# Modulation rows on another queue and in other places, and several orders of issue, in a two-layer trunk

## The chip, the cores and the metric

The kernel runs on one core of a Trainium2 chip. The metric is the device time of one execution in microseconds: three timed runs of the kernel before gave 3098.6, 3098.68 and 3101.12, median 3098.68. One more execution was taken with the profiler on. A core has a matmul engine (TensorE, PE in the profile; its weight loads are PEld), VectorE (DVE), ScalarE (ACT), GpSimd (POOL) and a queue engine (SyncE, SP) that here only starts transfers. Each engine runs its own instructions in the order written for it; transfers started by SP, ScalarE and GpSimd stand in one queue for each of them.

## The reference, cut to what matters

512 tokens of width 1024 pass a recurrent layer and an attention layer, each followed by a layer of small experts. Six vectors of 1024 for each of the two layers, and two for the shared keys and values, come from a condition vector and modulate the norms and the residuals:

```python
mod = (silu(c) @ ada_w[l] + ada_b[l])          # sh1, sc1, g1, sh2, sc2, g2
h = rmsnorm(x, norm_mix_g[l]) * (1.0 + sc1) + sh1
# l = 0: rglru_block: gate, rec = split(h @ w_in); xc = conv(rec)
#   r, i = sigmoid(xc @ wa + ba), sigmoid(xc @ wx + bx)
#   a = exp(-8 * r * softplus(-lam)); b = sqrt(1 - a**2) * i * xc
#   y = (gelu(gate) * scan(a, b)) @ w_out
# l = 1: mla_block, with keys and values from the same x and their own shift and scale
x = x + g1 * y
h = rmsnorm(x, norm_ffn_g[l]) * (1.0 + sc2) + sh2
x = x + g2 * peer(h)     # 8 heads: scores, top 16 of 128 x 128 experts, gelu(h.u), sum of v
```

## The kernel before, in words

Everything is kept transposed: 8 chunks of 128 features by 512 tokens. Matmuls work in three passes on a high and a low half of each operand. A weight tile is loaded by SP into a buffer `raw` (4 of them, L171 to L175), copied by ScalarE to its high half `whi` (3 buffers, L162), and what is left is subtracted to the low half `wlo` (3 buffers, L163), on VectorE or GpSimd.

The 14 vectors are 112 modulation rows of 128 x 1024 weights (0.5 MB each). `ada` (L143 to L152) loads a row on SP's queue and multiplies it with the condition on VectorE, which sums it to one column of `mod`. `adas(n)` takes the next n rows of the list `todo`. Rows 0 to 23 are done in the first products of the recurrent layer.

The order of the instructions on each engine is found by a planner that issues what is ready in its own timing, earlier program lines first. `issue_after(i)` puts what is traced under it, on the engine of `i`, behind `i`; `high_priority` puts it ahead of all else that is ready.

*Recurrent layer (`rglru`).* The record product (w_rec, 8 steps of 24 matmuls) runs while rows and norms are made; then gate products (w_in, L393 to L396), the convolution on VectorE (L384 to L389), gates and decays (L398 to L421). After two heads, the four roots are taken on ScalarE (L440), and products, scans and gates follow on VectorE (L442 to L449). 6 rows are put behind the convolution, 10 behind the last split. The output product (w_out, L454 to L463) ends with 8 residuals, squares and sums of squares; the sums (`nacc`, L226) are all on VectorE, and TensorE then adds them over the features (L232).

*Expert layer (`peer`).* Four score groups (pq) with top-16 searches on VectorE; 5 rows behind each in layer 0, 2 in layer 1, and expert products u (24 matmuls each) in between. Then 24 gate groups, 8 for each of three token blocks: one-hot matrices on VectorE and their matmuls (wps, L856). The gate tiles of the next block come from `decode` in 7 steps, the last of which ends in `gate_prep`. The fourth token block is done by gathers (L1146) on GpSimd's queue and VectorE, spread over all that follows. The value stage takes 128 steps: gate products on VectorE (L1020), splits of activations and of a value tile, 18 matmuls into six accumulators (`acc`); from step 84 on an expert product runs beside each step. In layer 0, rows are taken at every third step from step 2 on, up to row 67 (24 rows), and the rotary angles are computed at step 2 in the gathers' buffers. The last three steps are held back: first half, then second half in two parts with residuals between (`finish`).

*Attention (`mla`).* 16 heads; two rows after each head from the fourth on, up to row 87 (20 rows). The output product of each four heads adds a residual with rows 64 to 71. Layer 1's score groups take the last 8 rows.

## Time and profile before

| | us |
|---|---|
| median of three timed runs | 3098.68 |
| profiled execution, its own time | 3100.75 |
| its span, first to last instruction | 3098.8 |
| PE busy | 2980.4 (96%) |
| DVE busy | 2557.2 (83%) |
| ACT busy | 1381.6 (45%) |
| POOL busy | 860.2 (28%) |

The times in a profile are microseconds from the start of the span. A view by stretches gives, for each, its length, the busy time of each engine with its count of instructions, the granted clock of TensorE (1.00 is full) and what the transfers did. A view in order of time gives start, duration, engine, line, operation, output and inputs; in square brackets stands how long the engine had been idle before and what ended it. A view of waits gives the engine and line that waited, for whom, the sum, how often and the longest. The stages lie at: recurrent layer 0 to 212, score groups to 480, gate groups to about 790, value stage to 1500, attention to 1800, then the same expert stages to 3085.

### The profile page before, as it was taken

How to read it: one execution, taken by the hardware profiler on the slowest of the kernel's cores; microseconds unless marked ns; L12 is line 12 of the kernel's file. 1: busy time of each engine (PE TensorE's matmuls, PEld its weight loads, DVE VectorE, ACT ScalarE, POOL GpSimd, SP SyncE). 2: the span in 40 equal slices, each digit the busy share in tenths (PEclk: the TensorE clock that was granted, in tenths of full speed). 3: DMA queues.
4: the chain of work that ended last, by engine and by line, in shares of the span. 5: the costliest groups of instructions: out<-in, count | busy, mean ns of one | idle time of the engine just before them, and what ended most of it. 6: DMA issues, size and time to landing. Idle time of an engine off the chain costs nothing.

```text
span 3098.8 us, 43500 instructions
## 1 busy us (share of the span) xinstructions
PE 2980.4 (96%) x15516; PEld 2642.5 (85%) x15516; DVE 2557.2 (83%) x4841; ACT 1381.6 (45%) x1974; POOL 860.2 (28%) x667
## 2 busy tenths in 40 slices
PE   7889999999999999999899989999999999999998
PEld 5569999999877889998677779999999788889997
DVE  8789999898787878888767778999886787778886
ACT  5543255655333333333566642455554333333333
POOL 4000003343212215544333300014432221134441
PEclk9999999999999999999999999999999999999999
DMA  8344568999999999999313244469998999999994
GB/s 307 125 160 150 170 201 309 313 344 325 360 309 360 347 329 343 344 338 340 102 48 114 81 150 138 133 228 332 314 337 310 365 353 313 323 317 343 335 334 154
DMA packets 345047, 821.01 MB, mean 265 GB/s; under 512 B 33600, under 2 KB 179136, under 8 KB 338432
## 3 DMA queue, kind: packets, MB, share of 16 engines
q1 hardware_dynamic: 239632, 460.91, 44.2%
q0 software_dynamic: 73728, 268.47, 24.5%
q10 hardware_dynamic: 31472, 88.87, 7.4%
q8 instruction: 122, 2.00, 0.3%
q14 instruction: 93, 0.76, 0.1%
HBM read 730.85 MB, written 87.29 MB: 264 GB/s over the span
## 4 chain that ended last, share of the span: by engine, by line
PE 82%; DVE 7%; DMA 6%; issue 3%; ACT 2%; POOL 1%; DVEq 0%; ACTq 0%; SPq 0%; POOLq 0%
PE u L187 11%; PE u L188 11%; PE u L189 11%; PE acc L188 10%; PE acc L187 10%; PE acc L189 10%; PE wps L856 6%; PE pq L187 2%; PE pq L188 2%; PE pq L189 2%; DMA vraw<-in_v_dram 2%; DMA ada_raw<-in_adaw_dram 2%; DVE ada_junk L151 1%; PE sc L963 1%; DVE wlo L163 1%
## 5 line engine op out<-in xcount | busy, mean ns | idle before, releaser
L1146 POOL DMA_INDIRECT grow<-in_u_dram,idx x256 | 348.7, 1362 | 1280.0 <-DVE gdot L1150 441.0
L187 PE MATMUL u<-hh,wlo 128*128 128x384 f32 x2048 | 691.8, 338 | 1.5 <-ACT gsp L917 1.5
L189 PE MATMUL u<-hh,whi 128*128 128x384 f32 x2048 | 688.1, 336 | 0.0
L188 PE MATMUL u<-hl,whi 128*128 128x384 f32 x2048 | 686.6, 335 | 0.0
L188 PE MATMUL acc<-vl,ah 128*128 128x512 f32 x1536 | 598.6, 390 | 1.4 <-DVE vl L163 1.4
L189 PE MATMUL acc<-vh,ah 128*128 128x512 f32 x1536 | 598.4, 390 | 0.0
L187 PE MATMUL acc<-vh,al 128*128 128x512 f32 x1536 | 539.2, 390 | 17.7 <-ACT vh L162 9.1
L1146 POOL DMA_INDIRECT grow<-in_v_dram,idx x256 | 365.4, 1427 | 685.7 <-DVE gacc L1155 405.9
L163 DVE TENSOR_TENSOR wlo<-raw,whi 128x1024 fp32r<-128x1024 f32 x315 | 383.4, 1219 | 115.7 <-ACT whi L162 114.0
L163 DVE TENSOR_TENSOR vl<-vraw,vh 128x1024 fp32r<-128x1024 f32 x256 | 313.2, 1224 | 150.6 <-ACT vh L162 139.6
L162 ACT ACTIVATE whi<-raw 128x1024 fp32r<-128x1024 f32 (+2 forms) x372 | 358.6, 965 | 146.8 <-PE wo L189 27.7
L187 PEld LDWEIGHTS u<-hh,wlo 128*128 128x128 f32 x2048 | 386.5, 189 | 4.7 <-ACT gsp L917 1.8
L188 PEld LDWEIGHTS u<-hl,whi 128*128 128x128 f32 x2048 | 385.9, 188 | 2.7
L189 PEld LDWEIGHTS u<-hh,whi 128*128 128x128 f32 x2048 | 385.3, 188 | 0.0
L187 PEld LDWEIGHTS acc<-vh,al 128*128 128x128 f32 x1536 | 289.0, 189 | 80.8 <-ACT vh L162 11.3
L188 PEld LDWEIGHTS acc<-vl,ah 128*128 128x128 f32 x1536 | 289.4, 188 | 60.9 <-DVE vl L163 2.0
L189 PEld LDWEIGHTS acc<-vh,ah 128*128 128x128 f32 x1536 | 289.2, 188 | 59.7
L1155 DVE SCALAR_TENSOR_TENSOR gacc<-grow,gdot,gacc 128x1024 f32<-128x1024 f32 x254 | 324.8, 1279 | 12.2 <-DMA grow<-in_v_dram,idx 10.0
L162 ACT ACTIVATE vh<-vraw 128x1024 fp32r<-128x1024 f32 x256 | 268.9, 1051 | 141.1 <-DMA vraw<-in_v_dram 55.2
L1150 DVE CUSTOM_DVE_ANT_0 grow<-grow,hn 128x1024 f32<-128x1024 f32 x256 | 308.9, 1219 | 15.5 <-DMA grow<-in_u_dram,idx 15.4
L162 ACT ACTIVATE ah<-gact 128x384 fp32r<-128x384 f32 x180 | 94.1, 523 | 331.2 <-PE acc L189 168.8
L859 ACT ACTIVATE stg<-wps 128x512 f32<-128x512 f32 x192 | 187.7, 1110 | 49.2 <-PE wps L856 44.8
(352 smaller groups left out, 4203.5 us busy)
## 6 DMA issues: line engine op xcount, KB each, us to landing
raw<-in_uT_dram SPq DMA_DIRECT2D x256, 512.0 KB
vraw<-in_v_dram SPq DMA_DIRECT2D x256, 512.0 KB
ada_raw<-in_adaw_dram SPq DMA_DIRECT2D x112, 512.0 KB
wscr<-stg ACTq DMA_DIRECT2D x48, 1024.0 KB
wt<-wscr SPq DMA_DIRECT2D x32, 1536.0 KB
gscr<-gsp ACTq DMA_DIRECT2D x152, 192.0 KB
gact<-gscr SPq DMA_DIRECT2D x110, 192.0 KB
raw<-in_w_pq_dram SPq DMA_DIRECT2D x32, 512.0 KB
```

Source lines behind the costliest of these rows:

```text
L151: nc.vector.tensor_tensor_reduce(junk, raw, self.csil, op0=OP.mult, op1=OP.add, scale=1.0, scalar=b, accum_out=col)
L162: nc.scalar.activation(hi, src, AF.Copy)
L163: return (eng or nc.vector).tensor_tensor(lo, src, hi.bitcast(F32), op=OP.subtract)
L187: nc.tensor.matmul(out, al, bh, start=first, stop=False)
L188: nc.tensor.matmul(out, ah, bl, start=False, stop=False)
L189: return nc.tensor.matmul(out, ah, bh, start=False, stop=last)
L856: last = nc.tensor.matmul(wps[:, t * P:t * P + P], oo[:, n4 + a, :, t], pr[:, q * n4 + a, :, t], start=q == 0, stop=q == 1)
L859: nc.scalar.activation(stg[:, :, c:c + 4].rearrange("p e t -> p t e"), wps.rearrange("p (t e) -> p t e", t=4), AF.Copy, scale=1.0 / GSCALE)
L963: nc.tensor.matmul(sc[:, m * P:m * P + P], qs[m][:, b * P:b * P + P], keys[:, m, :], start=True, stop=True)
L1146: nc.gpsimd.indirect_dma_start(out=row, out_offset=None, in_=tabs[s], in_offset=bass.IndirectOffsetOnAxis(ap=idx[:, k:k + 1], axis=0))
L1150: nc.vector.tensor_tensor_reduce(row, row, hn, op0=OP.mult, op1=OP.add, scale=1.0, scalar=0.0, accum_out=col)
L1155: nc.vector.scalar_tensor_tensor(acc, row, col, acc, op0=OP.mult, op1=OP.add)
```

## The change

Rows: `ada` and `adas` get a queue; the 16 rows of the recurrent layer after the first 24 are loaded on GpSimd's queue, 8 behind the convolution and 8 behind the last split (before: 6 and 10 on SP's). Score groups of layer 0 take 6 rows instead of 5. In the value stage of layer 0 none is taken before step 64, then one every third step up to row 63 (16 rows, steps 66 to 111). So attention takes rows 64 to 87. The first two w_in tiles are loaded and split at high priority. The product after each root stands behind the last `a` of the decays. Four sums of squares of the recurrent layer go to GpSimd. The decode steps run one gate group ahead. The splits of value tiles 1 and 2 stand behind their step's gate product. The last three value steps of the second half are put so that five of the eight residuals stand between them (before: four).

```diff
-    def ada(self, n, pool=None, bufs=2):
+    def ada(self, n, pool=None, bufs=2, queue=None):
...
-        nc.sync.dma_start(raw, self.io["adaw"][n])
+        (queue or nc.sync).dma_start(raw, self.io["adaw"][n])
...
-            win = [self.wtile(io["w_in"][m], KC, eng=nc.vector) for m in range(2)]
+            with tc.high_priority():
+                win = [self.wtile(io["w_in"][m], KC, eng=nc.vector) for m in range(2)]
...
-                nc.vector.scalar_tensor_tensor(a, tt[j], 1.0, rr[j], op0=OP.add, op1=OP.mult)
+                self.last_a = nc.vector.scalar_tensor_tensor(a, tt[j], 1.0, rr[j], op0=OP.add, op1=OP.mult).ins
...
                 for j in js:
-                    nc.vector.tensor_tensor(tt[j], tt[j], rr[j], op=OP.mult)
+                    with tc.issue_after(self.last_a):
+                        nc.vector.tensor_tensor(tt[j], tt[j], rr[j], op=OP.mult)
...
             with tc.issue_after(conv):
-                self.adas(6, late, bufs=3)
+                self.adas(8, late, bufs=3, queue=nc.gpsimd)
             with tc.issue_after(lo):
-                self.adas(10, late, bufs=3)
+                self.adas(8, late, bufs=3, queue=nc.gpsimd)
...
-                self.sum_sq(t("sq"), self.x[:, m, :], m)
+                self.sum_sq(t("sq"), self.x[:, m, :], m, nc.gpsimd if m < KC - 3 else nc.vector)
...
-                        self.adas(5 if l == 0 else 2, pool)
+                        self.adas(6 if l == 0 else 2, pool)
...
-                    while ds < 7 * (i + 1) // nsg:
+                    while ds < 7 * (i + 2) // nsg:
...
-                vls.append(self.split(vh, vl, raw).ins)
+                with tc.issue_after(grp["i"].ins) if 0 < t < 3 else ExitStack():
+                    vls.append(self.split(vh, vl, raw).ins)
...
-                if t % 3 == 2 and l == 0:
-                    self.adas(1, stop=68)
+                if l == 0 and t >= 64 and t % 3 == 0:
+                    self.adas(1, stop=64)
...
-            for i, (t, pair) in enumerate(held):
-                with tc.issue_after(last):
-                    last = v_part(t, 1, *pair, 0, 2 * P)
-                if i:
-                    with tc.issue_after(last):
-                        last = finish(i - 1)
-            emit(1)
-            rest = [self.bank("rest")[:, :2 * P] for _ in range(nd)]
-            for i, (t, pair) in enumerate(held):
-                with tc.issue_after(last):
-                    last = v_part(t, 1, *pair, 2 * P, 2 * P, rest)
-                if i < 2:
-                    with tc.issue_after(last):
-                        last = finish(2 + i)
+            rest, c = None, 0
+            for q in range(2):
+                for i, (t, pair) in enumerate(held):
+                    with tc.issue_after(last):
+                        last = v_part(t, 1, *pair, 2 * q * P, 2 * P, rest)
+                    if q == 0 and i == LAST - 1:
+                        emit(1)
+                        rest = [self.bank("rest")[:, :2 * P] for _ in range(nd)]
+                    for _ in range((0, 2, 1, 1, 1, 0)[LAST * q + i]):
+                        with tc.issue_after(last):
+                            last = finish(c)
+                        c += 1
...
-                for c in range(4, KC):
+                for c in range(c, KC):
                     finish(c)
```

## Rows read from the trace of the kernel before

**Rows 1.** Waits of TensorE over the whole span: us in total, times, longest.

```profile
PE st L232 <- DVE nacc L226: 33.3, 7, 15.3
PE wps L856 <- DVE pr L849: 14.2, 6, 4.6
```

**Rows 2.** Stretches of 20 us: length, busy us (x instructions) by engine, clock, DMA.

```profile
120.00:140.00 20.00, 13.10 (x36) 6.78 (x35) 18.69 (x28) 13.01 (x20) 0.00 (x0) 0.91 0.25 93
...
200.00:220.00 20.00, 11.28 (x44) 9.09 (x45) 18.40 (x30) 11.49 (x18) 0.00 (x0) 0.66 0.71 263
...
680.00:700.00 20.00, 15.41 (x100) 15.06 (x99) 15.81 (x17) 8.56 (x12) 8.33 (x5) 0.91 0.85 314
...
2180.00:2200.00 20.00, 18.18 (x119) 17.94 (x120) 19.32 (x23) 11.42 (x14) 11.20 (x5) 0.91 0.87 269
```

**Rows 3.** TensorE in order of time, recurrent layer: start, us, instruction [idle before, releaser].

```profile
78.74 0.79 PE L187 MATMUL gate<-hmh,wlo 128*128 128x512 f32 x1 [4.02 <-DVE wlo L163]
...
133.27 3.54 PE L406 MATMUL ri<-xc,raw 128*128 128x512 f32 x4 [5.25 <-ACT gate L396]
138.47 0.50 PE L187 MATMUL gate<-hmh,wlo 128*128 128x512 f32 x1 [1.66 <-ACT g L408]
...
205.53 1.84 PE L232 MATMUL st<-ones,nacc 128*128 128x1 f32 x8 [6.93 <-DVE nacc L226]
...
211.68 1.65 PE L187 MATMUL pq<-hh,wlo 128*128 128x512 f32 x3 [1.63 <-ACT hh L272]
```

**Rows 4.** ScalarE and VectorE in order of time, recurrent layer.

```profile
73.00 1.16 ACT L162 ACTIVATE whi<-raw 128x1024 fp32r<-128x1024 f32 x1
...
77.46 1.22 DVE L163 TENSOR_TENSOR wlo<-raw,whi 128x1024 fp32r<-128x1024 f32 x1
...
128.51 0.72 ACT L440 ACTIVATE tanh<-tanh,tiny 128x512 f32<-128x512 f32 x1 [5.46 <-DVE a L419]
```

**Rows 5.** VectorE in order of time, end of the recurrent layer.

```profile
194.80 1.28 DVE L151 CUSTOM_DVE_ANT_0 ada_junk<-ada_raw,csil,vecs 128x1024 bf16<-128x1024 f32 x1 [1.05 <-DMA ada_raw<-in_adaw_dram]
...
202.45 0.74 DVE L282 SCALAR_TENSOR_TENSOR x<-wo,mod,x 128x512 f32<-128x512 f32 x1
```

**Rows 6.** SP's queue in order of time: start, us from first to last, issue.

```profile
16.19 0.33 SPq L512 DMA_DIRECT2D ps_pq<-in_posq_dram  x1
...
92.47 8.62 SPq L147 DMA_DIRECT2D ada_raw<-in_adaw_dram  x5
```

**Rows 7.** Longer stretches, same columns as rows 2: scores, value stages, attention.

```profile
212.00:480.00 268.00, 266.60 (x1458) 250.17 (x1458) 242.56 (x1010) 108.23 (x143) 4.63 (x4) 0.99 0.53 174
807.00:1000.00 193.00, 178.46 (x760) 143.23 (x760) 159.50 (x239) 65.31 (x86) 40.00 (x30) 0.98 0.98 345
1168.00:1400.00 232.00, 232.00 (x1175) 211.30 (x1175) 195.45 (x240) 83.33 (x116) 117.39 (x86) 1.00 0.98 345
1580.00:1780.00 200.00, 198.24 (x1051) 157.34 (x1050) 152.64 (x319) 132.16 (x311) 68.39 (x68) 1.00 0.28 88
2406.00:2600.00 194.00, 193.63 (x847) 160.24 (x848) 153.31 (x205) 69.35 (x97) 46.75 (x41) 0.99 1.00 349
```

**Rows 8.** Value accumulators, layer 0 and layer 1: ns min/median/max, first and last start.

```profile
L187 PE MATMUL acc<-vh,al x768: 277/389/792, 807.0 to 1496.4; 128*128 128x512 f32 x190, 128*128 128x256 f32 x2
...
L187 PE MATMUL acc<-vh,al x768: 278/389/764, 2406.4 to 3075.4; 128*128 128x512 f32 x190, 128*128 128x256 f32 x2
```

**Rows 9.** Row products, sums on GpSimd and gather issues, whole span, same columns.

```profile
L151 DVE CUSTOM_DVE_ANT_0 ada_junk<-ada_raw,csil,vecs x112: 1253/1278/1527, 13.4 to 2030.0; 128x1024 bf16<-128x1024 f32 x112
...
L226 POOL TENSOR_TENSOR nacc<-nacc,sqs x8: 1268/1286/1942, 1498.9 to 3082.6; 128x512 f32<-128x512 f32 x8
...
L1146 POOL DMA_INDIRECT grow<-in_v_dram,idx x256: 932/1028/4152, 522.5 to 3046.4; - x128
```

**Rows 10.** Waits of VectorE from 807 to 1000 us, same columns as rows 1.

```profile
DVE ada_junk L151 <- DMA ada_raw<-in_adaw_dram: 8.3, 4, 3.4
```

**Rows 11.** VectorE in order of time, the last residuals of layer 1.

```profile
3081.09 2.91 DVE L282 SCALAR_TENSOR_TENSOR x<-ot,mod,x 128x512 f32<-128x512 f32 x4
```

More of the change, by code (lines that the diff above doesn't have):

```diff
@@ L152, in ada, with adas @@
                                        accum_out=col)
-    def adas(self, n, pool=None, stop=112, bufs=2):
+    def adas(self, n, pool=None, stop=112, bufs=2, queue=None):
         while n and self.todo and self.todo[0] != stop:
-            self.ada(self.todo.pop(0), pool, bufs)
+            self.ada(self.todo.pop(0), pool, bufs, queue)
             n -= 1
```

## The prediction

> **What bounds the kernel now.** I read four views, in this order. The busy times say that TensorE works 2980.4 of 3098.8 us, so the time is the matmuls plus about 118 us in which TensorE stands, plus what a lowered clock costs after it has stood. So I read where it stands. The waits of the whole span [rows 1] put the largest on column sums that wait for the last sum of squares (33.3 us in 7 places) and on the gate matmuls that wait for their VectorE product (14.2 us in 6). The 20 us windows [rows 2] then show what each stall costs beside its wait: of 120 to 140 TensorE is idle 6.9 us and the clock is granted at 0.91, so 20 x 0.09 = 1.8 us more are lost; of 200 to 220 it is 0.66. The order in time [rows 3 to 6] shows, at each stall of the first layer, who was late. Last I set the two value stages beside each other, since they do the same matmuls: from the first to the last accumulation of the L187 form the first layer takes 1496.4 - 807.0 = 689.4 us and the second 3075.4 - 2406.4 = 669.0 us [rows 8]. The 20.4 us between them are the price of what only the first has in there: 24 modulation rows and the rotary angles.
>
> **The change part by part.** I count from the profiled execution's own time, 3100.75 us (span 3098.8 and 1.95 around it); the median of the timed runs, 3098.68, is 2.07 below.
>
> *Record stage: the first two w_in tiles at high priority.* TensorE waits 4.02 us at 78.74 for the low half of w_in[1] [rows 3]. Its high half was copied at 73.00 behind the record copies, and the low half came at 77.46 behind convolution work [rows 4]. Put ahead of both, it is ready some 4 us earlier, and the wait goes: 4.0 us. Below, it is worth 0 if VectorE, not TensorE, sets the end of this stage; above, 4.0 and about 0.8 of clock.
>
> *Roots.* ScalarE's fourth root stands 5.46 us, to 128.51, for the last `a` (L419) [rows 4], which VectorE reaches late because products of other columns (L442 to L444) were put ahead of it. ScalarE is in order, so a gate copy stands behind the root, a PSUM bank stays full, and TensorE waits 5.25 and then 1.66 us [rows 3]. With the products behind the last `a`, VectorE does its remaining `a` steps in a row, and most of the 5.46 goes. Worth: 6.9 us of wait and 1.8 of clock above, 0 below (the products are only moved, so VectorE's total is the same).
>
> *Rows on GpSimd's queue, 8 and 8 instead of 6 and 10; sums on GpSimd.* SP stands 8.62 us on five row loads at 92.47 [rows 6], and behind them the w_in loads. A load on GpSimd's queue keeps no weight load waiting. After the last split, VectorE takes the rows between 175 and 196; the last begins at 194.80 after waiting 1.05 for its load, and the residuals stand behind it: the last one begins at 202.45 [rows 5], though TensorE, which is then idle for 6.93 us before the sums at 205.53, had ended at 198.6 [rows 3]. Two rows fewer there are 2 x 1.28 us [rows 9], and four of the sums go to GpSimd, at 1.29 us each [rows 9], beside VectorE instead of on it. What must stay after the last matmul is residual, square and sum, each under 0.75 us, some 2.6 us with the hand-overs; so 6.93 - 2.6 = 4.3 us is the most that goes.
>
> Together the record stage could give 4.8 + 8.7 + 4.3 = 17.8 us. I take 10, because VectorE is nearly full there: once TensorE no longer stands, the y tiles of the second half become what is late, and VectorE gets two rows more (2.6 us) before them.
>
> *One row more in each of four score groups.* 4 x 1.28 = 5.1 us of VectorE between 212 and 480, where it has 268 - 242.6 = 25.4 us free and TensorE is at 266.6 of 268 [rows 7]. Cover: that free time. 0 to 5.1; I take 0.5.
>
> *Decodes one group earlier.* At a change of token block the gate tiles' decode is late: TensorE idle 4.6 us of 680 to 700, and 1.8 of 2180 to 2200, each with the clock at 0.91 [rows 2]; the second layer has another such place at 2280 of the same size. That is 4.6 + 1.8 + 2.0 and three times 1.8 us of clock, 13.8 us. Issuing the last step a whole gate group earlier (24 groups in the 300 us from 490 to 790, some 12 us each) covers each. VectorE does the same work. Range 0 to 13.8; I take 9, since the first block, whose decode is not moved, keeps its wait and each of the other stalls may leave a remainder.
>
> *Value stage.* None of the 24 rows stays in steps 2 to 65: 16 are loaded at steps 66 to 111, 4 in the score groups, 4 in attention. In 807 to 1000 TensorE is idle 193 - 178.5 = 14.5 us with a clock of 0.98 (some 3 us more), against 0.4 in the same stretch of the second layer; DMA shares are 0.98 and 1.00 [rows 7]. VectorE waits 8.3 us there for rows [rows 10], and what waits on VectorE in order is the value split. Some 15 rows (0.524 MB each) leave a stretch that moves 345 GB/s x 193 us = 66.6 MB: 12% less. The angles stay, and they hold the gathers' buffers, so the burst of gathers after them stays too. Range: 0 to 17.5 us; I take 9, half.
>
> *The rows' new place.* Of steps 66 to 111, those from 84 on run beside the expert products: TensorE is at 232 of 232, and 345 GB/s flow [rows 7]. Ten rows there are 5.24 MB in 232 us, 23 GB/s: 368 are wanted. The highest long stretch without a wait is 349 [rows 7]. If 368 flows, the cost is 0. If 349 is all there is, (368 - 349) / 349 x 232 = 12.6 us. I take 2, as the stretch at 349 had a share of 1.00 without TensorE waiting. The Trainium skill ("SBUF — State Buffer", Summary: rules for kernel authors) would have about 358 GB/s for HBM transfers; by it the cost would be 10 / 358 x 232 = 6.5 us, an estimate from that page, which no long stretch here contradicts.
>
> *Attention.* Rows 64 to 67 move in, so that its 20 become 24, and rows 64 to 71 are now made one head before the residuals that use them. VectorE has 200 - 152.6 = 47 us free [rows 7], so 4 x 1.28 is hidden; 0 to 5.1, I take 0.5.
>
> *Split order at steps 1 and 2* puts two value splits behind their gate product: a reorder of VectorE work of 1.2 us; -1 to +2, I take 0.
>
> *Last residuals.* Now four residuals follow the last accumulation (2.91 us), then the sums [rows 11]. Afterwards three: 0.73 us earlier in each layer; 0 to 3 for both, I take 1.5.
>
> Sum: -10 + 0.5 - 9 - 9 + 2 + 0.5 - 1.5 = -26.5; 3100.75 - 26.5 = 3074.25, forecast **3074 us**, 25 us (0.8%) below the median.
>
> **The rivals.**
>
> *A, slower: the early w_in tiles starve the record products.* An instruction whose operands are there is issued long before its place in the program: a load of the value stage goes out at 16.19 [rows 6]. The two w_in loads wait for nothing but a free buffer. At the front of the order they could be split before the first record tile and hold two of the three high and low buffers until 69 us. Then each of the seven later record steps waits for the step before, a copy (1.16) and a subtraction (1.22 [rows 4]), often behind a row product (1.28): 3.7 us, and after such a stall TensorE runs at half speed for a time (the matmul after the stall at 78.74 takes 0.79 us [rows 3], the median one 0.39 [rows 8]; about 1.5 us lost, an estimate): 5.2 x 7 = 36 us. Rows that VectorE does in those gaps give 6 back, and the 4.8 of the first edit is lost from the sum's 26.5: 36 - 6 - 21.7 = +8, **3109 us**. It turns the change slower from (21.7 + 6) / 7 = 4.0 us a step. Against it: with only the 3.7 us a step the change is level (3098), and no row shows how buffers are granted to work at high priority.
>
> *B, the parts overlap.* VectorE is the bound of the record stage and the angles, not the rows, that of the value stage: 3 us in each instead of 10 and 9, the gates 7. -3 - 7 - 3 + 3 - 1.5 = -11.5: **3089 us**. For it: VectorE is busy 159.5 of 193 us in the value stage's start [rows 7] and 18.7 of 20 at the roots [rows 2].
>
> *C, the late rows cost their full 12.6 us:* **3085 us**. For it: share 0.98 without them.
>
> *D, row loads on GpSimd's queue are issued slowly while VectorE works.* A gather issue took up to 4.15 us, the median being 1.03 [rows 9]; eight rows at 4.15 are 33 us, which from some 165 ends at 198, later than the 194.80 of now: the tail's 4.3 are lost and 3 more: **3082 us**. The Trainium skill ("SBUF — State Buffer", Who interferes with whom) names the cause: GpSimd shares its port with VectorE, and descriptors that it writes itself starve behind some VectorE instructions. By that rule this edit costs time, and the gathers' rows agree; but most gathers took a quarter of that.
>
> That an edit does nothing can hardly be: each changes the order of issue.
>
> **How the numbers follow.** Forecast 0.50, B 0.12, C 0.08, D 0.08, A 0.22 (half of it within 0.2%, at 3.7 us a step). About 0.2%, 6.2 us, is what a measurement of this kernel can tell from no change. Faster by more: 0.50 + 0.12 + 0.08 + 0.08, and a little of A: 0.79. Within: 0.09. Slower: 0.12. The forecast's own range is 3060 to 3087 (record stage -5 to -16, gates -5 to -14, value stage -4 to -17, late rows 0 to 8). The range to hold 8 in 10: from all the upper values that are likely together, 3052, to where A begins to cost, 3100.
>
> **What would show it.** Right: no wait of TensorE near 79 and 133; the first score product some 8 to 12 us before 211.68 [rows 3]; no dip of the clock at the two later block changes in both layers; the first value stage 8 us shorter than 689.4; TensorE still full in the stretch of steps 84 to 118. Wrong: w_in loads on SP's queue before 10 us and waits of the record matmuls for a low half (A); waits of TensorE between steps 84 and 111 (C); issues of row loads above 3 us and row products after the first residual (D); a first value stage as long as before (B).

## The result, and the profile after

The changed kernel took **3115.18 us** (median of five runs, 3113.17 to 3117.99) against 3098.68 in five runs of the kernel before beside it: ratio 1.0051, 95% interval 1.0037 to 1.0066. It is slower by some 16 us; 3074 had been forecast, with 3052 to 3100 as the range. The profiled execution took 3114.36 us, its span is 3112.6, 13.8 us more than before. All stage lengths below are from one profiled execution each. The stretch from the last value accumulation of the first layer to the second layer's scores (attention), in which these kernels differ little, took 304.7 to 311.9 us, so a difference of less than some 4 us in one stage is not read unless several profiles agree.

The starts of the first and last matmul of each stage place the 13.8 us:

| stage (first layer unless said) | before | after | difference |
|---|---|---|---|
| to the first score product | 211.7 | 207.9 | -3.8 |
| from there to the first gate matmul (wps) | 272.7 | 278.3 | +5.6 |
| gate stage, first to last wps | 293.2 | 303.4 | +10.2 |
| to the first value accumulation | 29.4 | 31.9 | +2.5 |
| value stage | 689.4 | 693.5 | +4.1 |
| all the rest: attention, second layer, end | 1602.4 | 1597.6 | -4.8 |

The waits of TensorE over the whole span of the changed kernel, to be held against [rows 1] (us in total, times, longest):

```profile
PE st L232 <- DVE nacc L226: 29.7, 7, 16.0
PE wps L858 <- DVE pr L851: 24.0, 12, 7.7
PE acc L187 <- ACT vh L162: 14.0, 1, 14.0
...
PE gate L187 <- ACT g L409: 5.6, 1, 5.6
...
PE gate L187 <- DVE wlo L163: 4.0, 1, 4.0
```

The sums' wait fell by 3.6 us. The gate matmuls wait longer (24.0 in 12 places, 14.2 in 6 before). New is a single wait of 14.0 us of a value accumulation for the high half of its tile, and the wait for w_in's low half, which was to go, is still there. Three stretches of 20 us show where that hurts (columns as in [rows 2]):

```profile
700.00:720.00 20.00, 17.64 (x116) 17.15 (x117) 18.34 (x17) 9.53 (x11) 10.90 (x7) 0.79 0.76 249
1480.00:1500.00 20.00, 8.80 (x39) 6.95 (x37) 15.69 (x15) 2.80 (x4) 11.69 (x9) 0.84 0.93 326
1500.00:1520.00 20.00, 15.53 (x94) 13.12 (x95) 14.75 (x17) 9.67 (x16) 5.01 (x5) 0.82 0.50 154
```

From 1480 on TensorE has stood for 11.2 of 20 us with the clock at 0.84, which is a mean over its two levels (1.2 and 2.4 GHz) in the stretch. The recurrent layer in order of time, TensorE, then ScalarE and GpSimd, answers to [rows 3, 4]:

```profile
79.37 0.50 PE L187 MATMUL gate<-hmh,wlo 128*128 128x512 f32 x1 [4.05 <-DVE wlo L163]
...
136.11 0.80 PE L187 MATMUL gate<-hmh,wlo 128*128 128x512 f32 x1 [5.57 <-ACT g L409]
...
201.66 1.02 PE L232 MATMUL st<-ones,nacc 128*128 128x1 f32 x8 [2.79 <-DVE nacc L226]
...
73.62 1.16 ACT L162 ACTIVATE whi<-raw 128x1024 fp32r<-128x1024 f32 x1
...
122.03 0.72 ACT L441 ACTIVATE tanh<-tanh,tiny 128x512 f32<-128x512 f32 x1 [0.37 <-DVE a L420]
130.79 0.63 ACT L162 ACTIVATE yh<-tanh 128x512 fp32r<-128x512 f32 x1 [3.11 <-DVE tanh L449]
133.64 1.83 ACT L162 ACTIVATE yh<-tanh 128x512 fp32r<-128x512 f32 x3 [2.22 <-DVE tanh L449]
...
183.62 0.53 POOL L147 DMA_DIRECT2D ada_raw<-in_adaw_dram  x1 [2.35 <-DVE mod L151]
193.31 5.42 POOL L226 TENSOR_TENSOR nacc<-nacc,sq 128x512 f32<-128x512 f32 x4 [9.17 <-ACT sq L225]
```

The fourth root now stands 0.37 us instead of 5.46. But ScalarE, in order, then stands 3.11 and 2.22 us on the copies `yh` of the gated scans, the gate copies L409 behind them are late, and TensorE waits 5.57 us at 136 where it waited 5.25 and 1.66. The tail gave what was counted: 6.93 became 2.79. The value accumulators (as [rows 8]) and the value stage's two stretches, shifted by 14 us, since the stage starts later (as [rows 7]):

```profile
L187 PE MATMUL acc<-vh,al x768: 278/389/792, 821.5 to 1515.0; 128*128 128x512 f32 x190, 128*128 128x256 f32 x2
...
821.00:1014.00 193.00, 189.17 (x829) 155.42 (x830) 156.39 (x231) 72.64 (x98) 40.81 (x31) 1.00 0.96 331
1182.00:1414.00 232.00, 230.92 (x1163) 209.10 (x1163) 193.69 (x245) 84.20 (x115) 108.40 (x78) 1.00 0.97 349
```

The early stall went as forecast: TensorE idle 3.8 us instead of 14.5 in the first 193 us. In the later stretch, where the rows now are, TensorE is full. But GpSimd, whose instructions here are the issues of the gathers, did 78 there; it did 86 before. VectorE, in the same two stretches, before and then after (busy us, mean ns | idle us just before them and for whom), did 86 products of gathered rows and then 76, with nine modulation rows in their place:

```profile
L1155 DVE SCALAR_TENSOR_TENSOR gacc<-grow,gdot,gacc 128x1024 f32<-128x1024 f32 x47 | 60.2, 1280 | 4.0 <-DMA grow<-in_v_dram,idx 3.5
L1150 DVE CUSTOM_DVE_ANT_0 grow<-grow,hn 128x1024 f32<-128x1024 f32 x39 | 47.0, 1219 | 2.3 <-DMA grow<-in_u_dram,idx 2.3
...
L1156 DVE SCALAR_TENSOR_TENSOR gacc<-grow,gdot,gacc 128x1024 f32<-128x1024 f32 x42 | 53.8, 1281 | 1.1 <-DMA grow<-in_v_dram,idx 0.9
L1151 DVE CUSTOM_DVE_ANT_0 grow<-grow,hn 128x1024 f32<-128x1024 f32 x34 | 40.9, 1220 | 1.9 <-DMA grow<-in_u_dram,idx 1.8
...
L151 DVE CUSTOM_DVE_ANT_0 ada_junk<-ada_raw,csil,vecs 128x1024 bf16<-128x1024 f32 x9 | 11.5, 1279 | 1.6 <-DMA ada_raw<-in_adaw_dram 1.6
```

The splits of the value tiles on VectorE (`vl`) tell when this costs time. The split of step 0 comes 11.7 us later than before (812.14, 800.47), that of step 84 only 0.8 us later (1168.81, 1168.04), that of step 120 1.7 (1460.75, 1459.06), and the last, of step 127, 18.2 (1508.55, 1490.31). So the late start of the stage is made good by step 84, and the loss comes in the last seven steps. VectorE, ScalarE and TensorE there, in order of time:

```profile
1486.01 1.28 DVE L1156 SCALAR_TENSOR_TENSOR gacc<-grow,gdot,gacc 128x1024 f32<-128x1024 f32 x1 [0.93 <-DMA grow<-in_v_dram,idx]
...
1495.43 1.29 DVE L1156 SCALAR_TENSOR_TENSOR gacc<-grow,gdot,gacc 128x1024 f32<-128x1024 f32 x1 [1.97 <-DMA grow<-in_v_dram,idx]
1497.77 3.92 DVE L1156 SCALAR_TENSOR_TENSOR gacc<-grow,gdot,gacc 128x1024 f32<-128x1024 f32 x3 [1.06 <-DMA grow<-in_v_dram,idx]
...
1501.73 1.06 ACT L162 ACTIVATE vh<-vraw 128x1024 fp32r<-128x1024 f32 x1 [12.46 <-DVE gacc L1156]
...
1502.84 1.65 PE L187 MATMUL acc<-vh,al 128*128 128x512 f32 x3 [14.04 <-ACT vh L162]
```

The last two value tiles are split into buffers of the gathers (`grow`, four of them). They can be had only when the gathers before them have been used up. So the 16 gathered rows that are accumulated between 1474.1 and 1506.8 come first, and TensorE stands. In the 34 us from 1474.1 on VectorE was busy for 29.1: 20.5 on these 16 sums, the rest on splits and gate products between them. It stood 4.4 us for rows that had not landed.

### The profile page after: what moved, and what is told of

Its sections match the earlier page's. It is cut to its first block, busy times and chain, and to the rows that moved or that the text cites. A ratio compares the mean times of both kernels' runs of the same rounds, so it can differ in the third digit from the quotient of the medians.

```text
span 3112.6 us, 43584 instructions
## 1 busy us (share of the span) xinstructions
PE 2982.2 (96%) x15516; PEld 2644.4 (85%) x15516; DVE 2555.6 (82%) x4837; ACT 1379.3 (44%) x1974; POOL 875.2 (28%) x687
## 4 chain that ended last, share of the span: by engine, by line
PE 71%; DVE 12%; issue 8%; DMA 6%; POOL 2%; ACT 1%; DVEq 0%; SPq 0%; ACTq 0%; POOLq 0%
PE acc L188 9%; PE acc L189 9%; PE acc L187 9%; PE u L187 9%; PE u L189 9%; PE u L188 9%; PE wps L858 5%; DMA ada_raw<-in_adaw_dram 2%; DVE wlo L163 2%; DMA grow<-in_v_dram,idx 1%; PE pq L187 1%; PE pq L188 1%; PE pq L189 1%; POOL grow L1147 1%; DVE ada_junk L151 1%
## 5 line engine op out<-in xcount | busy, mean ns | idle before, releaser
L188 PE MATMUL acc<-vl,ah 128*128 128x512 f32 x1536 | 598.3, 390 | 3.8 <-DVE vl L163 3.8
L187 PE MATMUL acc<-vh,al 128*128 128x512 f32 x1536 | 565.1, 389 | 20.4 <-ACT vh L162 14.0
L1156 DVE SCALAR_TENSOR_TENSOR gacc<-grow,gdot,gacc 128x1024 f32<-128x1024 f32 x254 | 325.2, 1280 | 17.5 <-DMA grow<-in_v_dram,idx 16.5
L1151 DVE CUSTOM_DVE_ANT_0 grow<-grow,hn 128x1024 f32<-128x1024 f32 x256 | 308.8, 1220 | 18.2 <-DMA grow<-in_u_dram,idx 18.0
L858 PE MATMUL wps<-pr,oo 128*128 128x128 f16 x1536 | 191.3, 297 | 24.2 <-DVE pr L851 24.0
```

The source lines that it names most:

```text
L187: nc.tensor.matmul(out, al, bh, start=first, stop=False)
L188: nc.tensor.matmul(out, ah, bl, start=False, stop=False)
L858: last = nc.tensor.matmul(wps[:, t * P:t * P + P], oo[:, n4 + a, :, t], pr[:, q * n4 + a, :, t], start=q == 0, stop=q == 1)
L1151: nc.vector.tensor_tensor_reduce(row, row, hn, op0=OP.mult, op1=OP.add, scale=1.0, scalar=0.0, accum_out=col)
L1156: nc.vector.scalar_tensor_tensor(acc, row, col, acc, op0=OP.mult, op1=OP.add)
```

## The experiments

Theory T: rows at steps 66 to 111 push gathers back in VectorE's order; they pile up at the end, and the last two value tiles wait for their buffers. Theory X: six rows in a score group and the earlier decode steps together make the gate stage longer. Rivals are named with each run. "Left" counts the gathers whose VectorE product (L1151 or L1156; 4 and 16 in the changed kernel) stands, in VectorE's order, between the value splits of steps 120 and 127, and "120 to 127" is the time between these two splits; "scores to values" is from the first score product to the first value accumulation.

| kernel | us | ratio to before, interval | scores to values | value stage | left | 120 to 127 |
|---|---|---|---|---|---|---|
| before | 3098.7 | | 595.3 | 689.4 | 11 | 31.2 |
| after | 3115.2 | 1.0051 (1.0037 to 1.0066) | 613.6 | 693.5 | 20 | 47.8 |
| e1 record stage alone | 3095.7 | 0.9994 (0.9985 to 1.0003) | 598.3 | 687.2 | 11 | 31.3 |
| e2 all but the rows | 3097.1 | 0.9998 (0.9988 to 1.0007) | 597.7 | 690.2 | 11 | 31.3 |
| e3 rows alone | 3114.6 | 1.0050 (1.0035 to 1.0065) | 598.2 | 696.6 | 21 | 50.2 |
| e4 decode alone | 3096.2 | 0.9992 (0.9983 to 1.0001) | 599.5 | 690.0 | 11 | 31.3 |
| e5 after, rows at 36 to 81 | 3097.1 | 0.9991 (0.9982 to 1.0000) | 613.2 | 682.3 | 13 | 35.3 |
| e6 after, old decode | 3102.2 | 1.0010 (1.0001 to 1.0019) | 600.7 | 693.6 | 20 | 47.9 |
| e7 e5 and e6 | 3098.1 | 0.9996 (0.9986 to 1.0005) | 599.0 | 683.8 | 13 | 34.5 |
| e8 after, other buffers | 3120.8 | 1.0072 (1.0058 to 1.0086) | 613.8 | 695.5 | 10, and 10 behind | 27.2 |
| e9 six rows and decode | 3107.0 | 1.0023 (1.0014 to 1.0032) | 605.2 | 693.5 | 11 | 31.2 |
| e10 after, rows at 81 to 126 | 3123.6 | 1.0075 (1.0061 to 1.0088) | 612.8 | 702.1 | 22 | 55.0 |
| e11 after, gathers early | 3098.8 | 0.9996 (0.9985 to 1.0007) | 612.3 | 675.9 | 6 | 24.1 |
| e12 eight rows | 3103.4 | 1.0014 (1.0004 to 1.0023) | 625.4 | 673.0 | 11 | 31.3 |
| e13 e11, old decode | 3092.2 | 0.9980 (0.9971 to 0.9989) | 600.7 | 684.7 | 6 | 23.8 |
| e14 e7, gathers a little early | 3094.7 | 0.9988 (0.9979 to 0.9996) | 602.2 | 690.9 | 6 | 24.0 |
| e15 e11 again | 3097.5 | 0.9998 (0.9989 to 1.0006) | 612.4 | 677.9 | 6 | 24.1 |

The last column goes with the count of gathers left, whatever else differs: 24 us with 6 of them, 27 with 10, 31 with 11, 34 to 35 with 13, 48 to 50 with 20 or 21, 55 with 22. From the split of step 84 to that of step 120 all kernels take 289.4 to 295.4 us.

### Which part: e1 to e4

e1 is the kernel before with the four record-stage edits:

```diff
+            with tc.high_priority():
+                win = [self.wtile(io["w_in"][m], KC, eng=nc.vector) for m in range(2)]
...
+                    with tc.issue_after(self.last_a):
+                        nc.vector.tensor_tensor(tt[j], tt[j], rr[j], op=OP.mult)
...
+                self.adas(8, late, bufs=3, queue=nc.gpsimd)
...
+                self.sum_sq(t("sq"), self.x[:, m, :], m, nc.gpsimd if m < KC - 3 else nc.vector)
```

> The four edits of the record stage alone on the kernel before (w_in at high priority, products behind the last a, 16 rows on GpSimd's queue, four sums on GpSimd). Theory R (the stages add up): the first score product comes 3.8 us earlier than before (at about 208) and all that follows keeps its length, so about 3095 us. Rival S (a change of order anywhere re-arranges the gate stage by chance, and the loss of 12.7 us there comes with any edit ahead of it): the first score product comes earlier too, but the stretch from the first score product to the first accumulation is longer than the 595 us of before by 5 us or more, so 3100 or above.

The first score product came at 206.5 and the time at 3095.7: theory R's number, but its interval holds no change. "Scores to values" is 3 us longer, between the two theories.

e2 is the changed kernel with the rows where they were:

```diff
-                        self.adas(6 if l == 0 else 2, pool)
+                        self.adas(5 if l == 0 else 2, pool)
...
-                if l == 0 and t >= 64 and t % 3 == 0:
-                    self.adas(1, stop=64)
+                if t % 3 == 2 and l == 0:
+                    self.adas(1, stop=68)
```

> All of the change but the rows' new places (5 rows in each score group, 24 rows in the value stage from step 2 on, as before). Theory T (rows at steps 66 to 111 push the gathers back, and the last two value tiles wait 14 us for their buffers): no wait of the last accumulations on a value split, and the early stalls of the value stage back; value stage about 688 instead of 693.5 us. Theory U (the sixth row of each score group made the score and gate stages longer): from the first score product to the first accumulation about 595 instead of 613.6 us. Both: about 3093 us. If the decode edit made the gate stages longer (theory V): the stretch stays above 605 and the time at 3105 or above.

e3 is the opposite, the kernel before with these two edits of the change alone:

```diff
-                        self.adas(5 if l == 0 else 2, pool)
+                        self.adas(6 if l == 0 else 2, pool)
...
-                if t % 3 == 2 and l == 0:
-                    self.adas(1, stop=68)
+                if l == 0 and t >= 64 and t % 3 == 0:
+                    self.adas(1, stop=64)
```

> Only the rows are moved on the kernel before: 6 in each score group, 16 at steps 66 to 111, 24 in attention. Theory T: the last accumulations of the first layer wait some 14 us for a value split, while the early stalls go: value stage about 693 us against 689.4. Theory U: from the first score product to the first accumulation some 610 us against 595, so in all about 3115. Theory V (decode edit to blame for the gate stage): this stretch stays within 3 us of 595, so about 3103.

e4 is the kernel before with the decode edit alone:

```diff
-                    while ds < 7 * (i + 1) // nsg:
+                    while ds < 7 * (i + 2) // nsg:
```

> Only the decode steps run one gate group ahead, on the kernel before. Theory V (the decode edit made the gate stages longer): the gate stage of the first layer takes about 303 instead of 293 us, so about 3108. Theory U (the sixth row did): the gate stages keep their length or lose the stalls at the block changes, 3092 to 3099. My prediction's step would give 3092.

Without the rows' move the rest of the change is level with the kernel before (e2), and the rows' move alone costs as much as the whole change (e3: 1.0050, the change 1.0051). In e3 TensorE waits as in the changed kernel:

```profile
1494.61 1.65 PE L187 MATMUL acc<-vh,al 128*128 128x512 f32 x3 [15.54 <-ACT vh L162]
```

Theory U, that the sixth row lengthens the stages before the values, falls: in e3 the gate stage begins 5.5 us later, but is as much shorter (287.7 against 293.2), since TensorE does expert products meanwhile. Theory V alone falls too: with the decode edit alone the gate stage is 296.8, not 303, and the time does not rise. e3's six runs lie between 3105.9 and 3122.4, and its profile is of one at 3108.1, so its stages account for half of its median's loss only. How much the rows' move costs alone is therefore not sure: e6 below has it together with the record stage's edits, at the old pace of the decode steps, and is only some 3 us slower than the kernel before.

### The late rows: e5, e8, e10, e11

e5, the changed kernel with the rows 30 steps earlier:

```diff
-                if l == 0 and t >= 64 and t % 3 == 0:
+                if l == 0 and t >= 36 and t % 3 == 0:
```

> The changed kernel, its 16 rows at every third value step from 36 on (36 to 81) instead of 66 on (66 to 111). Theory T (rows beside the expert products take VectorE's time from the gathers, and the last two value tiles stand in the gathers' buffers): by step 120 some 168 gathers are done again (160 in the changed kernel), the 14 us wait goes and with it some 4 us of clock; first value stage 672 to 680 us, total about 3098. Rival W (the wait comes from too few rows early, that is from 16 rows anywhere in this stage being too late): the wait stays above 8 us. The gate stage keeps its 303 us by either.

The long wait is gone, 13 gathers are left, and the time is 3097.1, as T had it; the value stage, 682.3, is a little longer than the 672 to 680 expected. Rival W falls.

e8, the rows as late as in the change, but the last two tiles in the weight buffers:

```diff
-                if t < P - 2:
+                if t < P:
                     vh = self.wp.tile([P, D], F32R, name="vh", tag="whi")
```

> The changed kernel, rows as late as there, but the last two value tiles of each value stage are split into the weight buffers (whi, wlo) like all others, not into the gathers' row buffers. Theory T: the wait of the last accumulations on the high half of a value tile goes or falls below 4 us; what is left comes as a wait of the transposes for the gathered sum, which still ends some 10 us late; and the next stage's first weights find no free buffer and come later by some us: about 3105 to 3112. Rival Z (the splits wait in VectorE's order behind the gathers' products, whatever their buffer): the wait stays at about 14 us, 3115.

The wait left the accumulation, so the buffers made it, and rival Z falls. But it came back whole at the next place that needs the gathers, the transposes of the gathered sum:

```profile
1514.30 0.47 PE L1099 MATMUL ot<-ident,gacc 128*128 128x128 f32 x1 [13.90 <-DVE gacc L1156]
```

With 3120.8 us it is a miss on the time (3105 to 3112). The lateness is that of the gathers, not of the buffers.

e10, the dose: all rows from step 81 on.

```diff
-                if l == 0 and t >= 64 and t % 3 == 0:
+                if l == 0 and t >= 81 and t % 3 == 0:
```

> The changed kernel with the 16 rows of the value stage at every third step from 81 on (81 to 126) instead of 66 on (66 to 111), so that 15 of them stand beside the expert products instead of 10. Theory T, by dose: each row there pushes back one gather; about 25 gathers (20 in the changed kernel) are left from step 120 on, the wait for the last two value tiles grows from 14 to some 20 us, total 3120 to 3124. Rival (the wait has a fixed size, set by the order of the last steps): 14 us again, 3115.

```profile
1507.52 1.65 PE L187 MATMUL acc<-vh,al 128*128 128x512 f32 x3 [20.74 <-ACT vh L162]
```

The wait (some 20 us expected) and the time (3120 to 3124) are as T had them. Only 22 gathers are left, not 25: VectorE takes 14 rows behind step 84 instead of 9, but two of them stand behind step 120 themselves, and the three others pushed back two gathers.

e11, the cure from the other side: rows as late, gathers earlier.

```diff
-            wts = [0.2 if t < KC else (0.45, 0.6)[l] if t < KC + SPILL else ...
+            wts = [0.2 if t < KC else (0.8, 0.6)[l] if t < KC + SPILL else ...
```

> The changed kernel, rows at steps 66 to 111 as there, with the gathers of layer 0 put earlier: weight 0.8 instead of 0.45 for steps 8 to 83, which by the goal's formula is some 20 gathers more before step 84. Theory T: by step 120 at most 10 gathers are left, the wait of the last value tiles falls from 14 to under 4 us, and the time to about 3100, if the earlier gathers find their transfers; rival W (the gathers cannot go earlier, as transfers or VectorE are full there too): waits of 5 us or more come back between steps 8 and 84 and the sum is 3108 or above.

VectorE's products of the gathered rows from step 120 on, in the changed kernel and then in e11 (ns min/median/max, first and last start; the second of the changed kernel says who waited for them):

```profile
L1156 DVE SCALAR_TENSOR_TENSOR gacc<-grow,gdot,gacc x16: 1278/1284/1286, 1474.1 to 1506.8; 128x1024 f32<-128x1024 f32 x16
...
  ACT vh L162: 13.1, 2
```

```profile
L1156 DVE SCALAR_TENSOR_TENSOR gacc<-grow,gdot,gacc x6: 1275/1278/1280, 1461.9 to 1482.7; 128x1024 f32<-128x1024 f32 x6
```

Six are left, the wait is 0.3 us, and the value stage falls to 675.9, near the second layer's 669 [rows 8]. Rival W of this run falls: the earlier stretch had room, for the transfers too (e11, columns as in [rows 2]):

```profile
915.00:1147.00 232.00, 228.16 (x1005) 188.05 (x1004) 194.85 (x272) 86.02 (x116) 74.70 (x61) 1.00 1.03 371
```

Time 3098.8, in e15 3097.5. So theory T stands, by a dose and by two cures. Beside the decode edit it is worth 1.0051 against 0.9991 to 0.9998, some 16 to 18 us. At the old pace of the decode steps the same cures give less: some 4 us from e6 to e7 (1.0010, 0.9996), some 9 from e6 to e13 (0.9980).

### The gate stage: e6, e7, e9, e12 to e15

e6, the changed kernel with the old pace of the decode steps; e7 is that with e5's edit too:

```diff
-                    while ds < 7 * (i + 2) // nsg:
+                    while ds < 7 * (i + 1) // nsg:
```

> The changed kernel with the decode steps at their old pace. Theory X (six rows and the earlier decode steps together: the rows move the gate stage's start, the decode steps then get in front of VectorE work that the expert products wait for): first score product to first accumulation back from 613.6 to about 598, total about 3099. Rival Y (the gate stage's loss has nothing to do with the decode edit, but with the order that the planner finds after any edit ahead): it stays above 606, total 3108 or more. The late wait of the value stage stays by either.

> The changed kernel with both: rows at steps 36 to 81 and the decode steps at their old pace. If theories T and X hold and add up: the record stage's 3.8 us stay, the value stage is 10 to 17 us shorter than before, about 3082. If only T: about 3098; if only X: about 3099.

e6 is as theory X had it: 613.6 fell to 600.7, and the ratio from 1.0051 to 1.0010. How the edit that was to bring the decode forward made it late, the last block change shows. The changed kernel, VectorE and then TensorE, in order of time:

```profile
687.23 0.22 DVE L814 TENSOR_TENSOR e<-oh 128x64 f32<-128x64 bf16 x1
...
700.74 1.29 DVE L851 TENSOR_TENSOR pr<-oo,gp 128x2048 f16<-128x2048 f16 x1
...
694.01 0.27 PE L822 MATMUL et<-ident,e 128*128 128x128 f32 x1
...
702.08 1.12 PE L858 MATMUL wps<-pr,oo 128*128 128x128 f16 x8 [7.70 <-DVE pr L851]
```

and e6:

```profile
672.01 0.22 DVE L814 TENSOR_TENSOR e<-oh 128x64 f32<-128x64 bf16 x1
...
687.16 2.35 DVE L851 TENSOR_TENSOR pr<-oo,gp 128x2048 f16<-128x2048 f16 x2
...
676.98 0.29 PE L822 MATMUL et<-ident,e 128*128 128x128 f32 x1
...
688.44 0.76 PE L858 MATMUL wps<-pr,oo 128*128 128x128 f16 x5 [0.96 <-DVE pr L851]
```

With the edit the last piece of the decode (`e`) comes 201 us after the first gate matmul (486.2), without it 189 us after (483.1). TensorE has begun two expert products by then (at 685.6), and the transposes `et` stand behind them until 694. The program's place of a decode step is not VectorE's place: the planner chose.

e7 is 3098.1, not 3082: its profile has both gains (599.0 and 683.8), its time is e5's. The profiled execution, 3093.8, is at the low end of its eleven runs (3090.65 to 3103.78); in it the last value split comes 14.0 us before e5's (1482.64, 1496.67), and what follows is 7.7 us longer. Where the median loses the gain is not shown. e9 asks whether six rows and the decode edit suffice, on the kernel before:

```diff
+                        self.adas(6 if l == 0 else 2, pool)
...
+                    while ds < 7 * (i + 2) // nsg:
...
+                    self.adas(1, stop=64)
```

(the rows of the value stage at every third step from 2 on).

> The kernel before with two edits only: 6 rows in each score group and the decode steps one gate group ahead; its 20 rows of the value stage stay at every third step from 2 on. Theory X (six rows and earlier decode steps together make the gate stage longer): first score product to first accumulation about 610 us against 595, with a stall of 7 to 8 us at the last block change, total 3108 to 3114. Rival Y (it takes the record stage's edits too): about 596 to 600, total 3095 to 3099.

605.2, a stall of 6.10 us at the last block change, and 3107.0 us: some half of X's 18 us, and just under its 3108. So the pair does it, and something else in the change adds to it; which is open.

e12 was to use the free score groups further: on the kernel before, the record-stage edits, the last residuals, 8 rows in each score group, 8 at steps 48 to 69.

```diff
+                        self.adas(8 if l == 0 else 2, pool)
...
+                if l == 0 and t >= 48 and t % 3 == 0:
+                    self.adas(1, stop=64)
```

> A version that draws on the runs so far: the record stage's edits and the order of the last residuals as in the change, decode steps at their old pace, 8 rows in each score group, the other 8 at value steps 48 to 69. If a row in a score group costs nothing as long as the decode steps keep their pace: first score product to first accumulation about 598, no late wait, value stage 676 to 684, total 3086 to 3094. If VectorE is full by 8 rows: that stretch grows by 5 to 10 us, 3098 to 3104.

A miss for the hoped-for side. The value stage is the shortest of all (673.0), but scores to values is 30 us longer, and there is a 7.69 us stall at the last block change without any decode edit. The first gate matmul waits for VectorE:

```profile
506.60 1.70 PE L858 MATMUL wps<-pr,oo 128*128 128x128 f16 x13 [8.54 <-DVE pr L851]
```

So four more rows were hidden there, twelve were not, and a late decode does not need the decode edit.

e13 takes e11 and the old decode pace, e14 takes e7 and a weight of 0.6, e15 is e11 once more, all beside each other:

```diff
 e13
+            wts = [0.2 if t < KC else (0.8, 0.6)[l] if t < KC + SPILL else ...
+                    while ds < 7 * (i + 1) // nsg:
 e14
+            wts = [0.2 if t < KC else (0.6, 0.6)[l] if t < KC + SPILL else ...
+                    while ds < 7 * (i + 1) // nsg:
+                if l == 0 and t >= 36 and t % 3 == 0:
```

> The changed kernel with the gathers of layer 0 early (weight 0.8) and the decode steps at their old pace. If the gate stage's loss reaches the end: first score product to first accumulation about 601 instead of 612 us, the value stage stays at 676 us, and the time is 10 to 13 us below that of the same kernel with the decode edit beside it, about 3086. If something later eats it (as the pair with rows at 36 to 81 hinted): the stretch is shorter all the same, but the time is within 3 us of the other's, about 3097.

> The changed kernel with the decode steps at their old pace, its 16 rows at steps 36 to 81, and the gathers of layer 0 a little earlier (weight 0.6 instead of 0.45). If the gate stage's gain reaches the end and VectorE has room between steps 36 and 84 for both: value stage 672 to 680 us, total 3084 to 3090. If VectorE or the transfers are full there: waits of 5 us or more between steps 36 and 84, total 3095 to 3100.

> The kernel with the gathers early (weight 0.8) and the decode edit once more, to stand beside the one without the decode edit on the same chip: 3098.8 us again (3096 to 3101), first score product to first accumulation 612 us.

e13 is faster than the kernel before by 0.2% (0.9980, at most 0.9989). Of the 11.7 us that its gate stage gains on e15, 6.8 are given back in its value stage, and 5.3 reach the end. SP's queue, ScalarE and TensorE of e13 show one place where:

```profile
1134.02 8.74 SPq L1061 DMA_DIRECT2D gsp<-gscr  x2
...
1143.33 0.38 SPq L1033 DMA_DIRECT2D vraw<-in_v_dram  x1
...
1155.03 1.06 ACT L162 ACTIVATE vh<-vraw 128x1024 fp32r<-128x1024 f32 x1 [7.54 <-DMA vraw<-in_v_dram]
...
1156.14 2.07 PE L187 MATMUL acc<-vh,al 128*128 128x512 f32 x4 [4.24 <-ACT vh L162]
```

A value tile, that of step 82, came late. Its load went out behind two others that held SP's queue for 8.74 us, and it was there 11.7 us later; meanwhile the transfers had little room (share 0.99 from 806 to 1150, half of the stage). But e15 has the same share and a stand of 6.96 us in SP's queue at the same step, and TensorE waited only 0.75 us. And five gathers more fall into e13's value stage, since 76 instead of 81 were done before it. Which of these costs the 6.8 us is not shown. e14 has such waits at 991 and 1031 (3.48 and 5.29 us), with 690.9 us for the stage: earlier gathers and rows at 36 to 81 do not both fit. This was the other side of e14's bet, with the time (3094.7) just under its 3095.

## Why the prediction was wrong

- **The rows' new place (+2, at most 12.6) is the step that failed.** I asked whether the transfers could carry 368 GB/s there, found them nearly able, and TensorE was indeed full in that stretch (230.9 of 232 us at 349 GB/s); e11, with 371 GB/s over 232 us, shows that more can flow than either limit I weighed. Nothing there waits in sight. What gave way was the work that nobody waits for yet, the gathers: VectorE did 10 fewer of their products in the stretch and nine rows instead, 9 more gathers were left at step 120, and the last seven splits took 16.6 us longer (47.8, 31.2), since the last value tiles, or else the gathered sum (e8), need them. In the time that is 16 to 18 us beside the decode edit (e5, e11) and 4 to 9 at the old pace (e7, e13). My term had no price for VectorE's time there. I had named the gathers' buffers only for the early burst. The rows of the trace that should have warned stand in [rows 7]: GpSimd's 86 instructions in the same 232 us, all of them gather issues.
- **Decodes (-9, 0 to 13.8) failed in sign:** alone 0 within the interval (e4), with six rows 12 to 14 us from scores to values, of which 13 us (after to e6), 5 (e15 to e13) or nothing (e5 to e7) came back in the time. I took an edit of the program's order for an edit of VectorE's order; the stall at the last block change went from 4.6 to 7.7 us. The two of the second layer, which were to go as well, are 1.42 and 2.33 us, after 2.00 and 1.96.
- **The record stage (-10) was mis-sized:** -3.8 in this profile. The first score product comes at 204.9 to 208.8 us in the 13 kernels with these edits, at 209.3 to 211.7 in the four without. The tail gave its 4.1 of 4.3. The roots' 6.9 turned into 5.6 of a later wait of the same engine. High priority did nothing: the copy of the second w_in tile, for which TensorE waits, is still behind the record copies, at 73.62 (73.00 before), and the wait is 4.05.
- **The score-group row (+0.5) was right** in the sum, by a mechanism I had not named: the gate stage starts 5.5 us later, by the full price, and TensorE does expert products in the time. It holds for four rows without the decode edit, not for twelve.
- **The value stage's start (-9) was right:** from the split of step 0 to that of step 84 it is 356.7 us instead of 367.6, and with the late wait cured the stage is 689.4 - 682.3 = 7.1 (e5) to 13.5 us (e11) shorter. In the changed kernel it is hidden under the loss at its end.
- **The last residuals (-1.5):** from the last accumulation of the second layer to the end it was 23.1 and is 22.0 us, and 21.6 to 23.2 in the others with this edit: too little to tell from nothing.
- **The rivals.** A had the sign, but not the mechanism: no record product waited for its low half, and no w_in load went early. B's 3 us for the record stage was near what came (3.8), its 3 for the value stage's start was not (10.9). C was the right place with the wrong resource: it charged the transfers at most 12.6 us in the stretch itself. D did not happen: the issue of a row on GpSimd took 0.53 us (median of 16, the longest 0.78), and the sums over the features came earlier (201.66, 205.53 before). The rule of the Trainium skill that was weighed there ("SBUF — State Buffer", Who interferes with whom) would have made these issues starve behind some VectorE instructions; no row of this run shows it.

What stays open: why the planner puts the gathers and the last decode later in its order (VectorE's time or the transfers' in its own reckoning), what besides the six rows and the decode edit makes the last 8 us from scores to values, and why the gains of the two cures do not add up in the time (e7, e13).

## What to carry to other kernels

Before work is moved into a stretch that looks full but stall-free, look for the background work in it that has slack now and a deadline later, and count how much of it must be done by when; it gives way first, and the bill comes at the deadline. An edit of the program's order under a planner is only an order of wishes: check the instruction's place on its engine, not in the source. A gain in one stage can be lost in the next (e13: 6.8 of 11.7 us), so the time decides, and not the stage.

## What was not expected of the hardware

Transfers ran at 349 GB/s with a share of 0.97 for 232 us while TensorE stood for 1.1 us only, and in e11 at 371 GB/s with a share of 1.03 for 232 us while it stood for 3.8. A plain row load issued by GpSimd took 0.53 us (median of 16), also from 175 to 196, where VectorE was busy for 15.9 of 21 us; a gather there took 0.93 to 4.15, the median being 1.03 [rows 9]. The four sums on GpSimd took 5.42 us together.
